# RWKV recurrence of a two-layer trunk: both heads' alpha and r in one tile, the keys' scores and the state apart, diagonal blocks in two parts

## Chip, cores and metric

The kernel runs on one core of a Trainium2 chip. The metric is the device time of one execution in microseconds. A run gives one time; a profile comes from one further execution.

## What is computed

A trunk of two layers on x of 1024 positions by 1024 channels. The first layer (gated spatial mixing beside dilated attention) is not touched. The second is RWKV-7 time mixing with 16 heads of 64 channels: projections of shifted inputs, then a recurrence over all positions, a norm of its output, a gate and an output projection. The recurrence is the part that matters here:

```python
def step(state, inp):
    r_t, w_t, k_t, v_t, kk_t, a_t = inp
    sa = jnp.einsum('bhvk,bhk->bhv', state, -kk_t)
    state = (state * w_t[:, :, None, :]
             + sa[..., None] * (kk_t * a_t)[:, :, None, :]
             + v_t[..., None] * k_t[:, :, None, :])
    y_t = jnp.einsum('bhvk,bhk->bhv', state, r_t)
    return state, y_t
```

## The kernel before

Everything is float32. The kernel does the recurrence in 16 chunks of 64 positions, all heads at once: 8 tiles q of two heads e each, on the partitions 64e to 64e+63. Of a chunk, A holds its alphas (the decayed removal keys) and r, BK its betas and keys. `scores` multiplies BK with both halves of A; ScalarE copies the r half into MY and the alphas' half, the keys' scores, into the other head's rows of A, so that one product over 128 rows, `W`, gives A-times-state plus scores-times-values. `alphas` gives the matrix M, which goes to DRAM (MA, `store_M`).

(1 + M) has to be inverted for each pair of chunks b. `load_M` brings M back, laid out for VectorE, into Nt: the same 64 rows of 4 KB go to the partitions 0 to 63 and 64 to 127. `inverse_a` forms DN from Nt and the norms rn (L1134) and solves the 8x8 diagonal blocks row by row, t = 1 to 7 (L1140 product, L1142 sum). `inverse_d` copies the blocks out, `inverse_b` does the block rows (L1165 to L1172), called one part at a time as `ib`. `inverse_c` stores the result to DRAM (XT, L1179), `load_X` brings it back (L1187), `merge_x` transposes it (`mx`, L1193, result rt), `merge_a` and `merge_b` (L1205, L1218) complete the inverse X on TensorE.

Then the chunks follow each other: `W` (L1230) gives Ws, `U` (L1240) multiplies it with X and puts the result beside the values in UV, `state` (L1261) adds BKT times UV (L1264) to what `keep` has scaled on GpSimd, and `Yout` (L1274) forms the output. State and values of a chunk share a tile SV, whose value half is loaded from DRAM (`load_sv`, L1031); UV's is loaded by `load_uv` (L1022).

The order is written by hand, in three strings: SCAN_START, six times SCAN_STEP (two chunks and one pair each) and SCAN_END. Each word calls one of these functions, and every engine and SP's DMA queue take their instructions in exactly that order. Work runs ahead: while chunks c and c+1 are finished, scores and alphas of c+4 and c+5 are made, M of pair b+2 is loaded and its diagonal blocks are solved, and the inverse of pair b+1 is merged. Between these, `g` places pieces of the gate's projection (L942, weights wraw split into wh and wl, L105 and L106; its results leave by a store sg_d on ScalarE's queue), of which ones with other inputs begin with the loads xh and xl. Tiles come from rings with a fixed number of buffers. DMAs count on eight shared completion counters, handed out in turn, so a DMA waits until the last one on its counter has landed.

Of the kernel before, what the change touches and what calls it, by code (L numbers as in the profile page):

```python
# [959 lines left out]

class Rwkv:
# [13 lines left out]
    def norms(self):  # L975

        g, nc, pool = self.g, self.g.nc, self.pool
        self.rn = rn = pool.tile([P, NB, 32], F32, name="rn")
        for c2 in range(2):
            for e in range(2):  # L980
                for b in range(2):
                    l0 = ((2 * e + b) * 2 + c2) * 8
                    src = bass.AP(tensor=g.ss_d.tensor, offset=g.ss_d.offset + e * KT * S + c2 * 64 + 32 * b,
                                  ap=[[S, 8], [128, NB], [1, 32]])
                    nc.scalar.dma_start(rn[l0:l0 + 8], src)

    def reciprocals(self, i):
        nc, rn = self.g.nc, self.rn
        nc.vector.tensor_scalar(rn[0:64], rn[0:64], 1e-24, None, op0=OP.max)
        nc.vector.reciprocal(rn[0:64], rn[0:64])  # L990
        nc.vector.tensor_copy(rn[64:128], rn[0:64])

    def ring(self, name, c, n, shape):
        k = name, c % n
        if k not in self.rings:
            if k == ("A1", NA - 1):
                self.rings[k] = self.pool.tile(shape, F32, name="Ax", bufs=1)
            else:
                self.rings[k] = self.g.s4(shape, F32, name)
        return self.rings[k]  # L1000

    def load(self, c):
        g, nc = self.g, self.g.nc
        A = []
        for e in range(2):
            rows, rest = slice(64 * e, 64 * e + 64), slice(64 - 64 * e, 128 - 64 * e)
            t = self.ring(f"A{e}", c, NA, [P, KT, 2, CH])
# [2 lines left out]
            nc.sync.dma_start(t[rows], g.A_d[rows, c])  # L1010
# [2 lines left out]
        nc.sync.dma_start(BK, g.BK_d[:, c])
        self.T[c] = dict(A=A, BK=BK)

    def load_uv(self, c):
        g, nc, pool = self.g, self.g.nc, self.pool
        UV = pool.tile([P, 2, KT, CH], F32, name="UV", bufs=2)
        v = g.v_d[c * CH:(c + 1) * CH]
        for e in range(2):  # L1020
            r = 64 - 64 * e
            nc.sync.dma_start(UV[r:r + 64, e].rearrange("t q d -> t (q d)"), v[:, e])  # L1022
        self.T[c]["UV"] = UV

    def load_sv(self, c):
        g, nc, pool = self.g, self.g.nc, self.pool
        v = g.v_d[c * CH:(c + 1) * CH]
        SV = pool.tile([P, 2, KT, CH], F32, name="SV", bufs=3)
        for e in range(2):
            r = 64 - 64 * e  # L1030
            nc.sync.dma_start(SV[r:r + 64, e].rearrange("t q d -> t (q d)"), v[:, e])  # L1031
        self.T[c]["SV"] = SV

    def scores(self, c, qq):
# [5 lines left out]
        pm = g.bB([P, 2, 4, 2, CH], "pm")  # L1042
        qs = slice(4 * qq, 4 * qq + 4)
        for i in range(4):
            q = 4 * qq + i
            for e in range(2):
                r = slice(64 * e, 64 * e + 64)
                nc.tensor.matmul(pm[:, e, i].rearrange("p j t -> p (j t)"), BK[r, q].rearrange("p j t -> p (j t)"),
                                 A[e][r, q].rearrange("p j t -> p (j t)"), start=True, stop=True)
        nc.scalar.activation(t["MY"].rearrange("p (e q) t -> p e q t", e=2)[:, :, qs], pm[:, :, :, 1], AF.Copy)  # L1050
        for e in range(2):
            r = slice(64 - 64 * e, 128 - 64 * e)
            nc.scalar.activation(A[e][r, qs, 0], pm[r, e, :, 0], AF.Copy)
# [52 lines left out]
    def load_M(self, b2):  # L1106
# [4 lines left out]
        for par in range(2):  # L1111
            nc.sync.dma_start(Nt[64 * par:64 * par + 64], g.MA_d[b2].rearrange("k c q t s -> (k c q) t s"))
        self.T[2 * b2]["Nt"] = Nf, Nt

    def inverse_p(self, b2):

        nc, pool = self.g.nc, self.pool
# [6 lines left out]
                              self.rn[:, b2].rearrange("p (k t) -> p k t", t=8))  # L1124
        self.blank = Xf, D, Nd

    def inverse_a(self, b2):
# [5 lines left out]
        r = self.rn[:, b2].rearrange("p (k t) -> p k t", t=8)  # L1133
# [119 lines left out]

    def state(self, c):
        g, nc, t = self.g, self.g.nc, self.T[c]
        if c < NC - 1:
# [5 lines left out]
            for e in range(2):  # L1262
                r = slice(64 * e, 64 * e + 64)
                nc.vector.tensor_tensor(self.T[c + 1]["SV"][r, e], pd[r], self.T[c + 1]["SV"][r, e], OP.add)  # L1264

    def Yout(self, c):
# [3 lines left out]
        for q in range(KT):  # L1270
            for a, b, first in (("MY", "UV", True), ("A", "SV", False)):
                for e in range(2):
                    w = t[a][:, 8 * e + q] if first else t[a][e][:, q, 1]
                    nc.tensor.matmul(py[64 * e:64 * e + 64, q], w, t[b][:, e, q], start=first, stop=not first)  # L1274
# [267 lines left out]
```

## Time and profile before

| | |
|---|---|
| median of 3 runs | 1496.92 us (1494.61 to 1498.73) |
| the profiled execution | 1504.67 us, of which span 1502.9 us |
| mean granted TensorE clock in it | 0.943 of full |
| TensorE, VectorE busy in the span | 89%, 62% |
| first layer | up to about 500 us |
| projections of the second | to about 987 us |
| recurrence (start, six steps, end) | about 987 to 1357 us |
| output projection, its tail | about 1357 to 1503 us |

A profile shows one execution: busy time of each engine, what each instruction waited for, DMA issues and packets. Engines: PE is TensorE, DVE VectorE, ACT ScalarE, POOL GpSimd, SP the engine that issues most DMAs. A name with q (SPq) is that engine's instruction queue. In a row of the timeline stand start, duration, engine, line, operation, tiles, and in brackets how long the engine stood idle before and what ended it.

### The profile page before, as it was taken

The numbers are of one execution on the slowest core, as the hardware profiler recorded it, in microseconds if no ns is written. First come the engines' busy times: TensorE is split into PE (matmuls) and PEld (weight loads), VectorE is DVE, ScalarE is ACT, GpSimd is POOL, SyncE is SP. The second block draws the span as 40 slices with busy tenths as digits, with TensorE's granted clock in tenths as the row PEclk, the third lists the DMA queues.
The fourth block names the chain that finished last, engine by engine and source line by source line (L and its number), as shares of the span: only waits on it lengthen the run. The fifth ranks groups of instructions, "written<-read, shape, count | busy, mean of one in ns | idle before, by whom it ended". The sixth has DMA issues, their size and how long they took to land.

```text
span 1502.9 us, 28032 instructions
## 1 busy us (share of the span) xinstructions
PE 1330.6 (89%) x11237; PEld 1130.5 (75%) x11237; DVE 933.2 (62%) x1504; ACT 645.2 (43%) x1236; POOL 565.1 (38%) x381
## 2 busy tenths in 40 slices
PE   5899999799989999999998779998878888978877
PEld 5887788688887799878754447996667777768777
DVE  8752536653565337650897898134577778777884
ACT  4422535543553234552654654134444444453322
POOL 9750102130114412211542543024654444477751
PEclk9999999899999999999998989999988999978998
DMA  6386436340523434142385557338486666765412
GB/s 217 85 273 174 126 117 165 80 131 8 168 78 115 139 127 139 36 150 78 88 250 145 121 150 187 78 98 237 110 256 171 163 158 163 204 207 197 153 31 98
DMA packets 256083, 213.19 MB, mean 142 GB/s; under 512 B 80416, under 2 KB 216192, under 8 KB 255952
## 3 DMA queue, kind: packets, MB, share of 16 engines
q1 hardware_dynamic: 232576, 196.11, 45.1%
q10 hardware_dynamic: 23376, 15.27, 3.8%
q8 instruction: 89, 1.46, 0.4%
q14 instruction: 42, 0.34, 0.1%
HBM read 139.90 MB, written 71.43 MB: 141 GB/s over the span
## 4 chain that ended last, share of the span: by engine, by line
PE 50%; DVE 19%; DMA 10%; ACT 7%; issue 7%; POOL 4%; SPq 3%; ACTq 0%; DVEq 0%; POOLq 0%
PE pj L153 33%; DVE tm L1140 2%; PE pt L572 2%; PE pj L1454 2%; PE pj L711 1%; PE pj L942 1%; DMA Nt<-MA 1%; DMA sg_d<-XT 1%; PE py L1274 1%; PE op L580 1%; ACT wh L105 1%; ACT xm L736 1%; DVE xm L737 1%; PE sp L559 1%; PE sp L562 1%
## 5 line engine op out<-in xcount | busy, mean ns | idle before, releaser
L106 POOL TENSOR_TENSOR wl<-wraw,wh 128x1024 fp32r<-128x1024 f32 x38 | 93.7, 2467 | 164.1 <-ACT wh L105 152.3
L106 DVE TENSOR_TENSOR wl<-wraw,wh 128x1024 fp32r<-128x1024 f32 x46 | 72.2, 1574 | 101.2 <-ACT wh L105 53.4
L153 PE MATMUL pj<-hh,wh 128*128 128x512 f32 x320 | 127.3, 398 | 0.0
L153 PE MATMUL pj<-hh,wl 128*128 128x512 f32 x320 | 126.6, 396 | 0.0
L153 PE MATMUL pj<-hl,wh 128*128 128x512 f32 x320 | 126.6, 396 | 0.0
L105 ACT ACTIVATE wh<-wraw 128x1024 fp32r<-128x1024 f32 x84 | 88.1, 1055 | 67.4 <-DMA wraw<-in_w_in_even_dram 23.0
L153 PE MATMUL pj<-xh,wh 128*128 128x512 f32 x256 | 103.4, 406 | 2.5 <-ACT ks L789 2.4
L153 PE MATMUL pj<-xl,wh 128*128 128x512 f32 x256 | 103.1, 403 | 2.6 <-DVE xl L740 2.6
L153 PE MATMUL pj<-xh,wl 128*128 128x512 f32 x256 | 102.7, 401 | 0.3 <-POOL wl L106 0.3
L566 DVE CUSTOM_DVE_ANT_0 sc<-sp,tb 128x128 f32<-128x128 f32 (+3 forms) x64 | 48.2, 754 | 56.7 <-PE sp L562 48.7
L1454 PE MATMUL pj<-wh,yh 128*128 128x256 f32 x256 | 76.0, 297 | 5.6 <-DVE x L1458 4.1
L1454 PE MATMUL pj<-wh,yl 128*128 128x256 f32 x256 | 75.0, 293 | 4.5 <-POOL yl L106 4.5
L737 DVE SCALAR_TENSOR_TENSOR xm<-hT,pr,xm 128x512 f32<-128x512 f32 x56 | 50.0, 935 | 45.2 <-ACT xm L736 44.8
L153 PE MATMUL pj<-wh,hh 128*128 128x256 f32 x256 | 74.8, 295 | 2.8 <-ACT hh L265 2.5
L153 PE MATMUL pj<-wh,hl 128*128 128x256 f32 x256 | 75.1, 294 | 1.2 <-DVE hl L266 1.2
L153 PE MATMUL pj<-wh,yl 128*128 128x256 f32 x256 | 73.7, 288 | 1.9 <-POOL yl L624 1.9
L1454 PE MATMUL pj<-wl,yh 128*128 128x256 f32 x256 | 74.6, 291 | 0.0
L153 PE MATMUL pj<-wl,hh 128*128 128x256 f32 x256 | 74.3, 291 | 0.0
L153 PE MATMUL pj<-wh,yh 128*128 128x256 f32 x256 | 73.2, 286 | 1.1 <-ACT yh L623 1.1
L153 PE MATMUL pj<-wl,yh 128*128 128x256 f32 x256 | 72.8, 284 | 0.0
L153 PE MATMUL pj<-wh,xh 128*128 128x256 f32 x256 | 72.2, 282 | 0.2
L153 PE MATMUL pj<-wl,xh 128*128 128x256 f32 x256 | 72.2, 282 | 0.0
(323 smaller groups left out, 4131.2 us busy)
## 6 DMA issues: line engine op xcount, KB each, us to landing
wraw<-in_w_in_even_dram SPq DMA_DIRECT2D x28, 512.0 KB
tb<-tb SPq DMA_DIRECT2D x16, 512.0 KB
A_d<-AR SPq DMA_DIRECT2D x16, 512.0 KB
wraw<-in_rw_wg_dram SPq DMA_DIRECT2D x16, 512.0 KB
BK<-BK_d SPq DMA_DIRECT2D x16, 512.0 KB
A<-A_d SPq DMA_DIRECT2D x30, 256.0 KB
xt<-in_x_dram SPq DMA_DIRECT2D x8, 512.0 KB
dv<-vt SPq DMA_DIRECT2D x16, 256.0 KB
```

The source lines that it names most:

```text
L105: nc.scalar.activation(hi, raw, AF.Copy)
L106: sub.tensor_tensor(lo, raw, hi.bitcast(F32), OP.subtract)
L153: nc.tensor.matmul(ps, a(k), b(k), start=(n == 0), stop=(n == 3 * KT - 1))
L559: nc.tensor.matmul(sp[:, c0:c1], qs[:, b * P:(b + 1) * P], kh[:, c0:c1], start=True, stop=False)
L562: nc.tensor.matmul(sp[:, c0:c1], qs[:, b * P:(b + 1) * P], kl[:, c0:c1], start=False, stop=True)
L566: nc.vector.tensor_tensor_reduce(sc[:, :n], sp[:, :n], tb[:, off:off + n], 1.0, BIG, OP.add, OP.min, mn)
L572: nc.tensor.transpose(pt[:, j - j0, :], sc[:, j * P:(j + 1) * P], g.ident)
L580: nc.tensor.matmul(op[:, s0:QW], vt[:, j, :], pth[j // 4][:, j % 4, s0:QW], start=(j == 0), stop=False)
L711: nc.tensor.matmul(ps, x[:, 2 * kk + i, :], y[:, i, o:o + 512], start=(n == 0), stop=(n == 47))
L737: nc.vector.scalar_tensor_tensor(t, hT[kk, f][:, j, 0:512], g.pr[:, i, k:k + 1], t, op0=OP.mult, op1=OP.add)
L1140: nc.vector.tensor_tensor(tv, D[:, :, 0:t, 0:t], Nd[:, :, t, 0:t][:, :, None, :].to_broadcast([P, 4, t, t]), OP.mult)
L1454: nc.tensor.matmul(ps[:, i, :], u[:, k], v[:, k % 4], start=(k == 0 and j == 0), stop=(k == KT - 1 and j == 2))
```

## The change

- A becomes one tile for both heads, loaded by one DMA of 512 KB instead of two of 256 KB; the zeroed halves and their memsets go.
- The keys' scores get a product `keys` of their own, with a tile AK; `scores` multiplies with r alone. W becomes two products, `Wkeys` (AK times UV, word V) and `W` (alphas times state).
- The state has a tile S; the value loads of SV go. `keep` and the state's addition are one operation each instead of two. UV has three buffers instead of two. `Yout` does all products of one kind, then all of the other.
- The two loads of Nt become one, whose source is a pattern that takes the same 64 rows twice (step 0, 2 times).
- The diagonal rows 5 to 7 move from `inverse_a`, ahead of `mx`, to `inverse_d`, behind it.
- The norms are loaded and inverted when the last keys have been projected, on SP's queue instead of ScalarE's.
- The three strings are written anew.

```diff
-FT = ((("BK", 3), ("BK", 3), ("BK", 3)), (("Nt", 1), ("tm", 1), ("SV", 3)), (("UV", 2), ("UV", 2), ("SV", 3)))
+FT = ((("BK", 3), ("BK", 3), ("BK", 3)), (("Nt", 1), ("tm", 1), ("FX", 1)), (("UV", 3), ("UV", 3), ("UV", 3)))
...
 SCAN_STEP = (
-    "U0 al0 ib2 st0 al1 sM0 sv0 Y0 keep1 ib1 W1 sc0 uv0 sv1 ib1 U1 sc1 ib1 ld6 ic0 dec0 st1 lM0 Y1 g1 W2 gx1 keep2 "
+    "U0 V1 al0 ib2 st0 al1 sM0 uv0 Y0 keep1 ib1 W1 sc0 ib1 U1 V2 ak0 uv1 ld6 st1 sc1 ib1 ic0 dec0 Y1 lM0 W2 keep2 ip0 "
...
+        if j == 9:
+            norms(g)
...
+def norms(g):
...
+            for b in range(2):
+                l0 = ((2 * e + b) * 2 + c2) * 8
+                src = bass.AP(tensor=g.ss_d.tensor, offset=g.ss_d.offset + e * KT * S + c2 * 64 + 32 * b,
+                              ap=[[S, 8], [128, NB], [1, 32]])
+                nc.sync.dma_start(rn[l0:l0 + 8], src)
+    nc.vector.tensor_scalar(rn[0:64], rn[0:64], 1e-24, None, op0=OP.max)
+    nc.vector.reciprocal(rn[0:64], rn[0:64])
+    nc.vector.tensor_copy(rn[64:128], rn[0:64])
...
     def load(self, c):
         g, nc = self.g, self.g.nc
-        A = []
-        for e in range(2):
-            rows, rest = slice(64 * e, 64 * e + 64), slice(64 - 64 * e, 128 - 64 * e)
-            t = self.ring(f"A{e}", c, NA, [P, KT, 2, CH])
-            if c < NA:
-                nc.gpsimd.memset(t[rest, :, 1], 0.0)
-            nc.sync.dma_start(t[rows], g.A_d[rows, c])
-            A.append(t)
+        A = self.ring("A", c, NA, [P, KT, 2, CH])
+        nc.sync.dma_start(A, g.A_d[:, c])
         BK = self.pool.tile([P, KT, 2, CH], F32, name="BK", bufs=3)
         nc.sync.dma_start(BK, g.BK_d[:, c])
         self.T[c] = dict(A=A, BK=BK)
     def load_uv(self, c):
         g, nc, pool = self.g, self.g.nc, self.pool
-        UV = pool.tile([P, 2, KT, CH], F32, name="UV", bufs=2)
+        UV = pool.tile([P, 2, KT, CH], F32, name="UV", bufs=3)
         v = g.v_d[c * CH:(c + 1) * CH]
         for e in range(2):
             r = 64 - 64 * e
             nc.sync.dma_start(UV[r:r + 64, e].rearrange("t q d -> t (q d)"), v[:, e])
         self.T[c]["UV"] = UV
-    def load_sv(self, c):
-        g, nc, pool = self.g, self.g.nc, self.pool
-        v = g.v_d[c * CH:(c + 1) * CH]
-        SV = pool.tile([P, 2, KT, CH], F32, name="SV", bufs=3)
-        for e in range(2):
-            r = 64 - 64 * e
-            nc.sync.dma_start(SV[r:r + 64, e].rearrange("t q d -> t (q d)"), v[:, e])
-        self.T[c]["SV"] = SV
...
     def scores(self, c, qq):
-        g, nc = self.g, self.g.nc
-        t = self.T[c]
+        g, nc, t = self.g, self.g.nc, self.T[c]
         A, BK = t["A"], t["BK"]
         if qq == 0:
             t["MY"] = self.ring("MY", c, NY, [P, NHD, CH])
-        pm = g.bB([P, 2, 4, 2, CH], "pm")
-        qs = slice(4 * qq, 4 * qq + 4)
+        pm = self.pm[:, :, qq]
         for i in range(4):
             q = 4 * qq + i
             for e in range(2):
                 r = slice(64 * e, 64 * e + 64)
-                nc.tensor.matmul(pm[:, e, i].rearrange("p j t -> p (j t)"), BK[r, q].rearrange("p j t -> p (j t)"),
-                                 A[e][r, q].rearrange("p j t -> p (j t)"), start=True, stop=True)
-        nc.scalar.activation(t["MY"].rearrange("p (e q) t -> p e q t", e=2)[:, :, qs], pm[:, :, :, 1], AF.Copy)
-        for e in range(2):
-            r = slice(64 - 64 * e, 128 - 64 * e)
-            nc.scalar.activation(A[e][r, qs, 0], pm[r, e, :, 0], AF.Copy)
+                nc.tensor.matmul(pm[:, e, i], BK[r, q].rearrange("p j t -> p (j t)"), A[r, q, 1], start=True, stop=True)
+        nc.scalar.activation(t["MY"].rearrange("p (e q) t -> p e q t", e=2)[:, :, 4 * qq:4 * qq + 4], pm, AF.Copy)
+    def keys(self, c):
+        g, nc, t = self.g, self.g.nc, self.T[c]
+        t["AK"] = AK = self.ring("AK", c // 2, 3, [P, 2, KT, CH])[:, c % 2]
+        pk = g.bC([P, KT, CH], "pt")
+        for q in range(KT):
+            for e in range(2):
+                r, o = slice(64 * e, 64 * e + 64), slice(64 - 64 * e, 128 - 64 * e)
+                nc.tensor.matmul(pk[o, q], t["BK"][r, q, 1 - e], t["A"][r, q, 0], start=True, stop=True)
+        nc.scalar.activation(AK, pk, AF.Copy)
     def alphas(self, c):
         g, nc, t = self.g, self.g.nc, self.T[c]
         M = self.ring("M", c // 2, 2, [P, 2, KT, CH])
-        pa = g.bA([P, KT, CH], "ch")
+        pa = g.bC([P, KT, CH], "pt")
         for q in range(KT):
             for e in range(2):
                 r = slice(64 * e, 64 * e + 64)
-                nc.tensor.matmul(pa[r, q], t["A"][e][r, q, 0], t["BK"][r, q, e], start=True, stop=True)
+                nc.tensor.matmul(pa[r, q], t["A"][r, q, 0], t["BK"][r, q, e], start=True, stop=True)
         nc.scalar.activation(M[:, c % 2], pa, AF.Copy)
...
-        for par in range(2):
-            nc.sync.dma_start(Nt[64 * par:64 * par + 64], g.MA_d[b2].rearrange("k c q t s -> (k c q) t s"))
+        m = g.MA_d[b2]
+        nc.sync.dma_start(Nf[:, 0:1024], bass.AP(tensor=m.tensor, offset=m.offset, ap=[[0, 2], [1024, 64], [1, 1024]]))
...
         self.T[2 * b2]["inv"] = Nt, X, D, Nd, Xf
-        for t in range(1, 8):
+        self.diag(D, Nd, 1, 5)
+    def diag(self, D, Nd, t0, t1):
+        nc = self.g.nc
+        for t in range(t0, t1):
...
     def inverse_d(self, b2):
         nc = self.g.nc
         Nt, X, D, Nd, Xf = self.T[2 * b2]["inv"]
+        self.diag(D, Nd, 5, 8)
...
+    def Wkeys(self, c):
+        g, nc, t = self.g, self.g.nc, self.T[c]
+        self.pw = g.bA([P, KT, CH], "ch")
+        for q in range(KT):
+            for e in range(2):
+                o, r = slice(64 * e, 64 * e + 64), slice(64 - 64 * e, 128 - 64 * e)
+                nc.tensor.matmul(self.pw[o, q], t["AK"][r, q], t["UV"][r, e, q], start=q == 0, stop=False)
     def W(self, c):
         g, nc, t = self.g, self.g.nc, self.T[c]
-        pw = g.bA([P, KT, CH], "ch")
         for q in range(KT):
             for e in range(2):
-                nc.tensor.matmul(pw[64 * e:64 * e + 64, q], t["A"][e][:, q, 0], t["SV"][:, e, q], start=True, stop=True)
-        nc.scalar.activation(self.Ws, pw, AF.Copy)
+                o = slice(64 * e, 64 * e + 64)
+                nc.tensor.matmul(self.pw[o, q], t["A"][o, q, 0], t["S"][o, q],
+                                 start=False, stop=q == KT - 1)
+        nc.scalar.activation(self.Ws, self.pw, AF.Copy)
...
+    def new_S(self, c):
+        S = self.pool.tile([P, KT, CH], F32, name="S", bufs=3)
+        self.T[c]["S"] = S
+        return S
     def keep(self, c):
-        g, t = self.g, self.T[c]
+        g = self.g
         if c < NC - 1:
-            for e in range(2):
-                r = slice(64 * e, 64 * e + 64)
-                g.nc.gpsimd.tensor_tensor(self.T[c + 1]["SV"][r, e], t["SV"][r, e],
-                                          g.EC[r, :, c:c + 1].to_broadcast([64, KT, CH]), OP.mult)
+            S = self.new_S(c + 1)
+            g.nc.gpsimd.tensor_tensor(S, self.T[c]["S"], g.EC[:, :, c:c + 1].to_broadcast([P, KT, CH]), OP.mult)
     def state(self, c):
         g, nc, t = self.g, self.g.nc, self.T[c]
...
                 for e in range(2):
                     r = slice(64 * e, 64 * e + 64)
                     nc.tensor.matmul(pd[r, q], t["BKT"][:, q, r], t["UV"][:, e, q], start=True, stop=True)
-            for e in range(2):
-                r = slice(64 * e, 64 * e + 64)
-                nc.vector.tensor_tensor(self.T[c + 1]["SV"][r, e], pd[r], self.T[c + 1]["SV"][r, e], OP.add)
+            S = self.T[c + 1]["S"]
+            nc.vector.tensor_tensor(S, pd, S, OP.add)
...
-            for a, b, first in (("MY", "UV", True), ("A", "SV", False)):
-                for e in range(2):
-                    w = t[a][:, 8 * e + q] if first else t[a][e][:, q, 1]
-                    nc.tensor.matmul(py[64 * e:64 * e + 64, q], w, t[b][:, e, q], start=first, stop=not first)
+            for e in range(2):
+                nc.tensor.matmul(py[64 * e:64 * e + 64, q], t["MY"][:, 8 * e + q], t["UV"][:, e, q],
+                                 start=q == 0, stop=False)
+        for q in range(KT):
+            for e in range(2):
+                r = slice(64 * e, 64 * e + 64)
+                nc.tensor.matmul(py[r, q], t["A"][r, q, 1], t["S"][r, q], start=False, stop=q == KT - 1)
         nc.scalar.activation(self.Y[:, c % 2], py, AF.Copy)
```

Where the strings move instructions, three places show it. The first is SP's queue at the Nt load of a steady step (sizes are those of the target; the name is target<-source). Before:

```order
L1010 DMA A_9498<-A_d 64x1024
L1010 DMA A_9501<-A_d 64x1024
L1013 DMA BK<-BK_d 128x1024
L1179 DMA XT_139<-xm 1024x1x32 x2
L1112 DMA Nt<-MA_132 64x1024 x2
L1187 DMA X<-XT_139 32x16x32 x4
L1022 DMA UV<-v_d 64x512 x2
L1010 DMA A_9581<-A_d 64x1024
```

And now:

```order
L1001 DMA A<-A_d 128x1024
L1003 DMA BK<-BK_d 128x1024
L1170 DMA XT_139<-xm 1024x1x32 x2
L1098 DMA Nt<-MA_132 128x1x1024
L1178 DMA X<-XT_139 32x16x32 x4
L1001 DMA A<-A_d 128x1024
L1003 DMA BK<-BK_d 128x1024
L928 DMA wraw<-in_rw_wg_dram 128x8x128
```

The load keeps its place between XT's store and X's loads, as one DMA; behind X now stands the next A, where UV's load stood.

The second is VectorE in the same step, from the block rows to the diagonal blocks. Before:

```order
L1165 TENSOR_TENSOR tm<-Nt,xm 128x576
L1167 TENSOR_REDUCE R<-tm 128x2x12
L1170 TENSOR_TENSOR tm<-DN,R 128x768
L1172 TENSOR_REDUCE xm<-tm 128x12x8
L1264 TENSOR_TENSOR SV<-ch,SV 64x512 x2
L106 TENSOR_TENSOR wl<-wraw,wh 128x1024
L1134 TENSOR_TENSOR DN<-Nt,rn 128x256
```

And now:

```order
L1156 TENSOR_TENSOR tm<-Nt,xm 128x576
L1158 TENSOR_REDUCE R<-tm 128x2x12
L1267 TENSOR_TENSOR S<-ch,S 128x512
L1161 TENSOR_TENSOR tm<-DN,R 128x768
L1163 TENSOR_REDUCE xm<-tm 128x12x8
L106 TENSOR_TENSOR wl<-wraw,wh 128x1024
L1120 TENSOR_TENSOR DN<-Nt,rn 128x256
```

The step's second addition to the state stands ahead of the last pair of row operations, after which XT is stored, instead of behind it.

The third is TensorE at the same place. Before, with the two A tiles taking turns in `scores` (eight rows in all behind U, of which two are shown):

```order
L1048 MATMUL pm<-A_9501,BK 128x128
L1240 MATMUL ch<-Ws,X 64x64 x16
L1048 MATMUL pm<-A_9498,BK 128x128
L1048 MATMUL pm<-A_9501,BK 128x128
...
L1261 MATMUL ch<-UV,BKT 64x64 x16
```

And now:

```order
L1029 MATMUL pm<-A,BK 128x64 x8
L1241 MATMUL ch<-Ws,X 64x64 x16
L1223 MATMUL ch<-UV,AK 64x64 x16
L1040 MATMUL pt<-A,BK 64x64 x16
L1265 MATMUL ch<-UV,BKT 64x64 x16
L1029 MATMUL pm<-A,BK 128x64 x8
```

Between U and the state's product (L1261, now L1265) stood half of a chunk's scores; now V (L1223) and the keys' product (L1040) stand there.

More of the change, by code (lines that the diff above doesn't have):

```diff
@@ L958, in pieces @@
                 yield
+def norms(g):
+    nc = g.nc
+    g.rn = rn = g.consts.tile([P, NB, 32], F32, name="rn")
+    for c2 in range(2):
+        for e in range(2):
[7 more added lines that the diff above has]
+    nc.vector.tensor_copy(rn[64:128], rn[0:64])
 class Rwkv:
@@ L973, in __init__ @@
         self.Ws = pool.tile([P, KT, CH], F32, name="Ws")
-    def norms(self):
-        g, nc, pool = self.g, self.g.nc, self.pool
-        self.rn = rn = pool.tile([P, NB, 32], F32, name="rn")
-        for c2 in range(2):
-            for e in range(2):
[L981 to L991, printed above, removed]
     def ring(self, name, c, n, shape):
@@ L995, in ring @@
         if k not in self.rings:
[L996 to L999, printed above, removed]
+            self.rings[k] = self.g.s4(shape, F32, name)
         return self.rings[k]
@@ L1095, in masks @@
                                     base=0, channel_multiplier=-1)
-        for e in range(2):
-            ak = t["A"][e][64 - 64 * e:128 - 64 * e, :, 0]
-            nc.gpsimd.affine_select(ak, ak, pattern=[[0, KT], [1, CH]], compare_op=OP.is_ge, fill=0.0,
+            nc.gpsimd.affine_select(t["AK"][r], t["AK"][r], pattern=[[0, KT], [1, CH]], compare_op=OP.is_ge, fill=0.0,
                                     base=-1, channel_multiplier=-1)
@@ L1123, in inverse_p @@
         nc.gpsimd.tensor_copy(D.rearrange("p k c t -> p k (c t)")[:, :, 0:64:9],
-                              self.rn[:, b2].rearrange("p (k t) -> p k t", t=8))
+                              g.rn[:, b2].rearrange("p (k t) -> p k t", t=8))
         self.blank = Xf, D, Nd
@@ L1132, in inverse_a @@
         X = Xf[:, 0:512].rearrange("p (c t) -> p c t", t=32)
[L1133 removed]
+        r = g.rn[:, b2].rearrange("p (k t) -> p k t", t=8)
         nc.vector.tensor_tensor(Nd, Nf.rearrange("p (k z) -> p k z", z=264)[:, :, 0:256]
@@ L1261, in state @@
                     nc.tensor.matmul(pd[r, q], t["BKT"][:, q, r], t["UV"][:, e, q], start=True, stop=True)
-            for e in range(2):
-                r = slice(64 * e, 64 * e + 64)
-                nc.vector.tensor_tensor(self.T[c + 1]["SV"][r, e], pd[r], self.T[c + 1]["SV"][r, e], OP.add)
+            S = self.T[c + 1]["S"]
+            nc.vector.tensor_tensor(S, pd, S, OP.add)
     def Yout(self, c):
@@ L1270, in Yout @@
         for q in range(KT):
-            for a, b, first in (("MY", "UV", True), ("A", "SV", False)):
-                for e in range(2):
-                    w = t[a][:, 8 * e + q] if first else t[a][e][:, q, 1]
-                    nc.tensor.matmul(py[64 * e:64 * e + 64, q], w, t[b][:, e, q], start=first, stop=not first)
+            for e in range(2):
+                nc.tensor.matmul(py[64 * e:64 * e + 64, q], t["MY"][:, 8 * e + q], t["UV"][:, e, q],
+                                 start=q == 0, stop=False)
+        for q in range(KT):
+            for e in range(2):
+                r = slice(64 * e, 64 * e + 64)
+                nc.tensor.matmul(py[r, q], t["A"][r, q, 1], t["S"][r, q], start=False, stop=q == KT - 1)
         nc.scalar.activation(self.Y[:, c % 2], py, AF.Copy)
@@ L1285, in zs @@
         def zs(i):
-            for e in range(2):
-                nc.gpsimd.memset(self.T[0]["SV"][64 * e:64 * e + 64, e], 0.0)
-        ops = dict(nm=self.reciprocals, L=gate.load, wx=gate.split, xl=gate.load_x, ld=self.load,
+            nc.gpsimd.memset(self.new_S(0), 0.0)
+        self.pm = g.bB([P, 2, 2, 4, CH], "pm")
+        ops = dict(L=gate.load, wx=gate.split, xl=gate.load_x, ld=self.load,
                    g=lambda i: [next(gate.rest, None) for _ in range(i)],
@@ L1294, in start @@
                    dec=self.decayed, T=self.transposed, msk=self.masks,
-                   sv=self.load_sv, uv=self.load_uv, W=self.W, keep=self.keep, zs=zs)
+                   ak=self.keys, uv=self.load_uv, V=self.Wkeys, W=self.W, keep=self.keep, zs=zs)
         for name, i in order(SCAN_START):
@@ L1302, in ops @@
             U=lambda i: self.U(c + i), st=lambda i: self.state(c + i), keep=lambda i: self.keep(c + i),
-            W=lambda i: self.W(c + i), sc=lambda i: self.scores(c + 4 + i // 2, i % 2),
+            W=lambda i: self.W(c + i), V=lambda i: self.Wkeys(c + i), sc=lambda i: self.scores(c + 4 + i // 2, i % 2),
             al=lambda i: self.alphas(c + 4 + i), sM=lambda i: self.store_M(b + 2 + i),
@@ L1311, in ops @@
             T=lambda i: self.transposed(c + 4 + i), Y=lambda i: self.Yout(c + i),
-            msk=lambda i: self.masks(c + 4 + i), sv=lambda i: self.load_sv(c + 2 + i),
+            msk=lambda i: self.masks(c + 4 + i), ak=lambda i: self.keys(c + 4 + i),
             uv=lambda i: self.load_uv(c + 2 + i), ld=lambda i: c + i < NC and self.load(c + i),
```

6 lines of the change are left out of this document (2 added, 4 removed), and 12 rows, old and new, of tables (SCAN_END, SCAN_START).

## The prediction

> **What bounds the kernel now.** I read the page's totals and its chain first, then the waits, grouped, of the recurrence's steady part (1104 to 1342 us), then one step's timeline on VectorE and on SP's queue.
>
> ```profile
> PE 1330.6 (89%) x11237; PEld 1130.5 (75%) x11237; DVE 933.2 (62%) x1504; ACT 645.2 (43%) x1236; POOL 565.1 (38%) x381
> ...
> PE 50%; DVE 19%; DMA 10%; ACT 7%; issue 7%; POOL 4%; SPq 3%; ACTq 0%; DVEq 0%; POOLq 0%
> ```
>
> TensorE is busy for 89% of the span, but the chain that ended last runs through TensorE for only half of it. The change touches the recurrence alone (about 987 to 1357 us), so what counts is what that stage waits for:
>
> ```profile
> PE pt L1218 <- DVE rt L1193: 26.1, 7, 4.5
> ...
> DVE SV L1264 <- PE ch L1261: 11.0, 10, 1.9
> DVE DN L1134 <- DMA Nt<-MA: 7.3, 5, 2.6
> ```
>
> The columns are total us, times, longest. TensorE's one large wait is `merge_b` (L1218) for the transposed inverse `rt` (L1193, `merge_x`), some 4 us in each step. So VectorE is late. Why, the timeline of the step from 1201 to 1237 us tells (start, duration, engine, line):
>
> ```profile
> 1201.17 0.70 DVE L1193 STREAM_TRANSPOSE rt<-X 128x512 f32<-128x512 f32 x1
> ...
> 1217.52 0.95 DVE L1172 TENSOR_REDUCE xm<-tm 128x96 f32<-128x768 f32 x1
> 1217.60 1.23 SPq L1010 DMA_DIRECT2D A<-A_d  x2
> 1218.93 0.53 SPq L1013 DMA_DIRECT2D BK<-BK_d  x1
> 1219.56 1.39 SPq L1179 DMA_DIRECT2D XT<-xm  x2
> 1220.05 1.41 DVE L1264 TENSOR_TENSOR SV<-ch,SV 64x512 f32<-64x512 f32 x2 [1.57 <-PE ch L1261]
> 1221.00 4.21 SPq L1112 DMA_DIRECT2D Nt<-MA  x2
> 1228.26 0.61 DVE L1134 TENSOR_TENSOR DN<-Nt,rn 128x256 f32<-128x256 f32 x1 [1.57 <-DMA Nt<-MA]
> ...
> 1234.55 0.95 DVE L1140 TENSOR_TENSOR tm<-DN 128x100 f32<-128x100 f32 x1
> 1237.26 0.70 DVE L1193 STREAM_TRANSPOSE rt<-X 128x512 f32<-128x512 f32 x1
> ```
>
> This is a loop, one turn per step. After `mx` (1201.17) come the block rows of the inverse, until 1218.47 (17.3 us). SP stores XT at 1219.56 (1.1) and, behind it in its queue, issues the Nt load at 1221.00 (1.4). VectorE, in its fixed order, stands at DN until Nt has landed, 1228.26 (7.3), and does the diagonal blocks before the next `mx` at 1237.26 (9.0). Sum 36.1 us. `mx` feeds TensorE's `mb`, and the next turn starts. From the second to the seventh `mx` there are five turns:
>
> ```profile
> 1128.54 0.70 DVE L1193 STREAM_TRANSPOSE rt<-X 128x512 f32<-128x512 f32 x1
> 1305.51 0.70 DVE L1193 STREAM_TRANSPOSE rt<-X 128x512 f32<-128x512 f32 x1
> ```
>
> That is 177.0 us, 35.4 each. The Nt load lies on this loop, and nothing hides a longer one: DN and what follows are next in VectorE's order.
>
> **The change, part by part.** First the part that I hold to decide. The two Nt loads of 64 rows become one of 128 rows, whose source is written as 2 copies of 64 rows. How many of the 16 DMA engines a transfer gets can be counted by the small packets that complete it:
>
> ```profile
> DMA packets 8, 0.01 MB, mean 5 GB/s; under 512 B 4, under 2 KB 4, under 8 KB 8
> ...
> ss_d<-so SPq DMA_DIRECT2D x1, 4.0 KB
> bo_d<-so SPq DMA_DIRECT2D x1, 4.0 KB
> ```
>
> ```profile
> DMA packets 544, 0.26 MB, mean 52 GB/s; under 512 B 32, under 2 KB 544, under 8 KB 544
> ...
> v_d<-rt SPq DMA_DIRECT2D x2, 128.0 KB
> ```
>
> ```profile
> q10 hardware_dynamic: 72, 0.01, 2.4%
> ...
> rn<-ss_d ACTq DMA_DIRECT2D x3, 8.0 KB
> ```
>
> In a quiet window (948.4 to 950.2) two stores of two 2 KB rows make 4 data and 4 small packets: two completions each. Two v_d stores (969 to 974) make 32: sixteen each. One rn load (all that ACT's queue q10 moved from 1010 to 1014) has 64 runs of 128 B, 8 KB, and the 72 packets leave 8 completions. It has 64 rows at its source, yet its target is written as 8 groups of 8 rows. So the outermost step of a pattern, not its rows or bytes, bounds the engines: 2, 8, 16. The new load's source has 2 in its outermost step, so I forecast **two engines**, with 64 rows of 4 KB each, where sixteen had 8 each in all.
>
> The page "DMA: Bandwidth & Descriptors" of the Trainium skill, section "Why a DMA increments its semaphore by 16 and not by 1", says the same as a rule: the engine count is the largest number up to 16 that divides the outermost dimension larger than one of both patterns, here of 128 and 2. That speaks against this change, and the three counts above agree with it; no run here shows it for a step of stride zero.
>
> What does an engine move in a microsecond?
>
> ```profile
> DMA packets 795, 2.90 MB, mean 414 GB/s; under 512 B 84, under 2 KB 88, under 8 KB 795
> ...
> q1 hardware_dynamic: 795, 2.90, 102.7%
> ```
>
> ```profile
> q1 hardware_dynamic: 484, 1.63, 96.3%
> ```
>
> From 13 to 20 us, loads of 4 KB rows keep sixteen engines full: 2.90 MB / 7 us / 16 = 25.9 GB/s each. From 1031 to 1038, with Nt and A loads, 1.63 MB / (7 us x 16 x 0.963) = 15.1 GB/s. An engine's share of the new load is 256 KB: 10.1 to 17.4 us, where an eighth of it took 1.3 to 2.2. **Added: 8.9 to 15.2 us per load.** I take 8.9: with fourteen engines idle it is nearer to the row without contention. The same page's "Specifications" gives some 27 GiB/s per engine; by that figure, an estimate, it would be 9.0 us per load instead of 10.1 and some 8 us less over the seven loads that count. The measured 25.9 decides.
>
> The loop's other terms in a steady step:
> - Rows: the last pair of row operations now stands behind the second state addition, and that behind W's key product V and the keys' product, which stand ahead of the state product on TensorE.
>
> ```profile
> 1216.11 1.15 PE L1240 MATMUL ch<-Ws,X 64*64 64x64 f32 x32
> 1217.69 1.16 PE L1048 MATMUL pm<-A,BK 64*128 64x128 f32 x16 [0.43 <-ACT A L1053]
> 1218.78 1.15 PE L1261 MATMUL ch<-UV,BKT 128*64 128x64 f32 x32
> ```
>
>   A group of 32 passes of 64x64 costs 1.15 us here, with 64 rows (first row) as with 128 (last). U ends at 1217.3; V and keys 2.3; state 1.15; the addition, now one 128x512 operation, 0.7 (half of the 1.41 above); the last pair 1.94: 1223.4, less 0.7 for the first addition, which is halved too: 1222.7, so 21.6 us after `mx` instead of 17.3. **+4.3.** Not hidden: the XT store waits for it. If V and keys ran in others' shadow, it would be +2.
> - XT issue: A and BK have been issued long before, 0.3 instead of 1.1: -0.8. XT to Nt stays 1.4.
> - Nt without the penalty: 7.3, of which the 2 us of A and BK issued just ahead no longer stand in front, nor the rest of that queue: 4.4 (3.5 to 7.3), -2.9.
> - Diagonal rows 5 to 7 go behind `mx`: 1237.26 - 1234.55 = 2.7 less. The remaining 6.3 hold operations that took 0.9 and more for a handful of elements while POOL worked; later in a longer step POOL has finished: 5.0 (4.6 to 6.3), -4.0 in all.
>
> Sum: 21.6 + 0.3 + 1.4 + 4.4 + 5.0 = 32.7 us, and with 8.9 for the two engines **41.6**. Against 35.4 that is +6.2, five times: **+31**.
>
> The start pays twice:
>
> ```profile
> 1038.24 1.49 DVE L1134 TENSOR_TENSOR DN<-Nt,rn 128x256 f32<-128x256 f32 x1 [13.99 <-DMA Nt<-MA]
> ...
> 1066.77 1.26 SPq L1179 DMA_DIRECT2D XT<-xm  x2
> 1068.21 1.31 SPq L1112 DMA_DIRECT2D Nt<-MA  x2
> 1070.40 2.17 SPq L1187 DMA_DIRECT2D X<-XT  x4
> 1075.02 0.71 DVE L1193 STREAM_TRANSPOSE rt<-X 128x512 f32<-128x512 f32 x1 [8.28 <-DMA X<-XT]
> ```
>
> VectorE stands idle 14 us for the first Nt, then works without a gap until XT goes out: +8.9 passes through. The second Nt stands ahead of the X loads in the same queue, and `mx` waits for X: on the two engines X's share comes behind Nt's, +8.9 again. The first `mx` moves from 1075.0 to 1092.8. From it to the second there were 53.5 us, 18.1 more than a turn, of which these waits go:
>
> ```profile
> ACT UV L1243 <- DMA xh<-xg: 7.9, 1, 7.9
> ...
> ACT MY L1050 <- DMA XT<-xm: 8.6, 1, 8.6
> ```
>
> ScalarE was held behind two stores of the gate, whose completion counters are shared with a load; the counters fall otherwise now. What is late next: wraw behind X, and A and BK behind the eight gate loads of 512 KB. I keep 10 of the 18 (3 to 18). The second `mx` comes at 1092.8 + 41.6 + 10 = 1144.4: **+16** (+6 to +25).
>
> The rest I cost at nothing:
>
> ```profile
> 1201.20:1237.30 36.10, 31.03 (x619) 26.38 (x619) 27.17 (x42) 16.99 (x32) 16.77 (x17) 0.91 0.64 166
> ...
> SPq L1022 <- PE py L1274: 80.8, 5, 17.4
> ```
>
> The first row is the same turn by engine (length, then PE's busy time, weight loads, DVE, ACT, POOL, then the granted clock, the DMA share and GB/s). SV's 32 loads, the memsets and SP's long wait for Y (second row) go, but they were off the loop: the queue held back loads, not VectorE. On TensorE, scores without the alphas' half save half of 1.16 us four times, 2.3; keys and V, two groups each per turn, add 4 x 1.15, 4.6: 31.0 becomes 33.3, hidden while a turn takes 41.6 and the bound if a turn could be shorter. From the last of the five turns to the tail no Nt load follows: -2 (-5 to +3) for the halved additions. The tail is unchanged.
>
> Sum: 31 + 16 - 2 = **+45** on the profiled execution's 1504.67 us (span 1502.9), so 1549.7. It ran 7.75 us above the median of 1496.92; taken off, **1542 us**.
>
> **Rivals.**
> 1. *All sixteen engines serve the load* (the outermost step of stride zero is folded away, or the target's 128 rows decide). For it: the loads before, of 64 rows, were short, and the trace has no transfer with a repeated source. Against it: rn, whose 8 rather than 64 set the count. The loop is then 32.7 us, so TensorE's 33.3 binds: -2.1 five times, -10.5; the start loses the two ScalarE waits in part, -8; the end -2: -20.5, 1476 us, **faster**. It decides from where seven loads eat that gain, 2.9 us more each than before: 512 KB in 4.2 us, that is five engines at 25.9 GB/s.
> 2. *Two engines, and slow ones*: 15.1 GB/s as from 1031 to 1038, where the same source rows were read. Then 6.3 us more per load, seven times: +44, 1586 us.
> 3. *The queue behind the load binds*: SP's next BK load waits for the completion counter that Nt uses, and A, BK, wraw and UV stand behind it. For it: SP's queue is in order. Against: they are wanted only in the next step's first products, some 6 us after `mx`. If 3 us late: +15, 1557 us.
>
> **How the numbers follow.** Forecast 0.61 (1517 to 1562: loop 39 to 44, start +6 to +25), rival 2 0.14, rival 3 0.10, rival 1 0.11, something between (some five engines, about no change) 0.04. The likeliest is 1542. The range leaves out rival 1 and the upper part of rival 2: 1508 to 1576. A measurement of this kernel can tell 0.3%, 4.5 us, from no change: faster 0.11, same 0.04, slower 0.85.
>
> **What would show it.** Right: VectorE's wait for Nt (DN, now L1120) of some 8 to 10 us in each step; stretches of ten us in which the DMA share is about a tenth or two (2 of 16 engines) while Nt is in flight; `mx` (L1184) 41 to 42 us apart, and TensorE's wait for it over 8 us; the first `mx` near 1093. An XT store 21 to 22 us after `mx` confirms the rows' term. Wrong: Nt landing within 5 us of its issue and `mx` 33 to 34 us apart (rival 1), or `mx` 48 apart (rival 2), or first products after `mb` waiting for BK or UV (rival 3).

## The result, and the profile after

The changed kernel takes 1544.34 us (median of 4 runs, 1541.35 to 1551.85) beside 1495.76 us before (4 runs, 1490.02 to 1498.73): ratio 1.0337, 95% interval 1.0288 to 1.0386. It is slower by some 49 us. The profiled execution took 1541.35 us. The ratios, here and below, are not the quotients of the two medians, and two executions at a low granted clock (1743 us at 0.69, 1962 us at 0.60) are not in them.

The page of the changed kernel, busy times and chain:

```profile
PE 1349.7 (88%) x12261; PEld 1154.1 (75%) x12261; DVE 885.2 (57%) x1489; ACT 631.7 (41%) x1188; POOL 545.9 (35%) x353
...
PE 57%; DVE 15%; DMA 10%; issue 5%; ACT 5%; POOL 3%; SPq 3%; ACTq 1%; DVEq 0%; POOLq 0%
PE pj L153 34%; PE pj L943 3%; DMA X<-XT 3%; SPq L1178 2%; PE pj L1460 1%; PE pt L572 1%; PE pj L711 1%; PE pm L1029 1%; DMA BK<-BK_d 1%; DMA Nt<-MA 1%; PE pt L1051 1%; PE sp L559 1%; PE ch L1241 1%; PE sp L562 1%; PE op L580 1%
```

VectorE and GpSimd do less than before, and the kernel is longer: the time is waited for. The chain now names the loads of X at 3% and SP's issuing of them (L1178) at 2%, which it did not before. The grouped waits of the recurrence (1104 to 1380 us; total, times, longest) say on what:

```profile
PE pt L1196 <- DMA X<-XT: 42.9, 8, 9.0
...
PE pt L1209 <- ACT rt L1199: 4.0, 2, 3.7
...
DVE DN L1120 <- DMA Nt<-MA: 64.8, 6, 11.5
DVE S L1267 <- PE ch L1265: 37.5, 12, 6.4
```

VectorE waits 64.8 us for Nt, where it was 7.3 for the five loads shown of before, and TensorE waits at `merge_a` (L1196) for X. A wait of TensorE's `merge_b` (L1209) for VectorE's transpose, 26.1 us before, is no longer among its waits; the 4.0 us at L1209 are for a copy on ScalarE. The turn of the loop from 1125.75 to 1169.05, on VectorE, SP and TensorE:

```profile
1125.75 0.70 DVE L1184 STREAM_TRANSPOSE rt<-X 128x512 f32<-128x512 f32 x1
...
1148.15 0.69 DVE L1267 TENSOR_TENSOR S<-ch,S 128x512 f32<-128x512 f32 x1 [5.86 <-PE ch L1265]
1149.74 0.95 DVE L1163 TENSOR_REDUCE xm<-tm 128x96 f32<-128x768 f32 x1
1150.72 1.27 SPq L1170 DMA_DIRECT2D XT<-xm  x2
1152.09 0.56 SPq L1098 DMA_DIRECT2D Nt<-MA  x1
1154.36 8.96 SPq L1178 DMA_DIRECT2D X<-XT  x4
1166.87 0.42 DVE L1120 TENSOR_TENSOR DN<-Nt,rn 128x256 f32<-128x256 f32 x1 [11.09 <-DMA Nt<-MA]
1167.41 0.28 PE L1196 MATMUL pt<-X,M 32*32 32x32 f32 x2 [8.41 <-DMA X<-XT]
1169.05 0.70 DVE L1184 STREAM_TRANSPOSE rt<-X 128x512 f32<-128x512 f32 x1
1174.25 1.20 PE L1209 MATMUL pt<-rt 32*32 32x32 f32 x64
```

Nt lands 14.8 us after its issue, where it was 7.3. Of X's four loads the first goes out 2.3 us behind Nt and the last 10.8 us: SP is 8.96 us at their issue, where it was 1.9 in the turn of before that the prediction shows. X is there some 1 us after Nt. How many engines carry Nt stands in the DMA view of 1157 to 1166 us, whose digits are the mean busy share of the 16 engines in tenths:

```profile
DMA  9899989811111111111111111101296693110111
GB/s 246 200 246 209 246 189 195 169 56 55 55 55 55 55 55 46 55 46 55 55 55 55 55 55 46 64 36 73 62 182 137 123 223 67 61 55 36 55 55 39
```

For some 4 us on end the queues move a steady 55 GB/s, at a share of one tenth, while Nt is in flight. Two of 16 engines full are 0.125, and 55 GB/s on two are some 27 each, beside the 25.9 that the forecast took from the row of 13 to 20 us.

### The profile page after: what moved, and what is told of

It reads as the page before. It is cut to its first block, busy times and chain, and to the rows that moved or that the text cites. A ratio compares the mean times of both kernels' runs of the same rounds, so it can differ in the third digit from the quotient of the medians.

```text
span 1539.6 us, 29856 instructions
## 1 busy us (share of the span) xinstructions
PE 1349.7 (88%) x12261; PEld 1154.1 (75%) x12261; DVE 885.2 (57%) x1489; ACT 631.7 (41%) x1188; POOL 545.9 (35%) x353
## 4 chain that ended last, share of the span: by engine, by line
PE 57%; DVE 15%; DMA 10%; issue 5%; ACT 5%; POOL 3%; SPq 3%; ACTq 1%; DVEq 0%; POOLq 0%
PE pj L153 34%; PE pj L943 3%; DMA X<-XT 3%; SPq L1178 2%; PE pj L1460 1%; PE pt L572 1%; PE pj L711 1%; PE pm L1029 1%; DMA BK<-BK_d 1%; DMA Nt<-MA 1%; PE pt L1051 1%; PE sp L559 1%; PE ch L1241 1%; PE sp L562 1%; PE op L580 1%
## 5 line engine op out<-in xcount | busy, mean ns | idle before, releaser
L1460 PE MATMUL pj<-wl,yh 128*128 128x256 f32 x256 | 75.5, 295 | 0.0
L153 PE MATMUL pj<-wh,xl 128*128 128x256 f32 x256 | 72.8, 284 | 0.0
```

What stands on the lines that cost most here:

```text
L153: nc.tensor.matmul(ps, a(k), b(k), start=(n == 0), stop=(n == 3 * KT - 1))
L1460: nc.tensor.matmul(ps[:, i, :], u[:, k], v[:, k % 4], start=(k == 0 and j == 0), stop=(k == KT - 1 and j == 2))
```

## The experiments

Each ran beside the kernel before, on the same chip. A turn below is the mean of the five from the second to the seventh transpose `mx` in the profiled execution.

**Two loads of 64 rows again.** In the changed kernel only this:

```diff
-        nc.sync.dma_start(Nf[:, 0:1024], bass.AP(tensor=m.tensor, offset=m.offset, ap=[[0, 2], [1024, 64], [1, 1024]]))
+        for par in range(2):
+            nc.sync.dma_start(Nt[64 * par:64 * par + 64], g.MA_d[b2].rearrange("k c q t s -> (k c q) t s"))
```

> The whole change, but Nt again loaded by two DMAs of 64 rows (as before the change). Theory (the one load runs on two DMA engines, and that is what costs): each of the two completes on 16 engines, Nt lands some 4 to 5 us after the issue of the first instead of 14.4, the merges (transposes of X on VectorE) come 33 to 35 us apart instead of 42.7, and the time is 1476 us, 1462 to 1490: faster than before the change. Rival (the rest of the change costs the time, later block rows, or W's second product): it stays above 1520, with merges over 40 us apart.

1495.0 us, ratio to before 0.9971 (0.9944 to 0.9999). The load explains all of the loss; but the time is above the expected range, and the rest of the change, for which 1476 was expected, gains only some 3 to 4 us. The same places of the loop, one turn from 1152.3 to 1188.07:

```profile
1173.45 0.69 DVE L1268 TENSOR_TENSOR S<-ch,S 128x512 f32<-128x512 f32 x1 [4.65 <-PE ch L1266]
...
1176.02 1.52 SPq L1171 DMA_DIRECT2D XT<-xm  x2
...
1177.64 1.27 SPq L1099 DMA_DIRECT2D Nt<-MA  x2
...
1182.60 0.52 DVE L1121 TENSOR_TENSOR DN<-Nt,rn 128x256 f32<-128x256 f32 x1 [1.53 <-DMA Nt<-MA]
...
1188.07 0.70 DVE L1185 STREAM_TRANSPOSE rt<-X 128x512 f32<-128x512 f32 x1
```

Nt lands 5.0 us after its issue, and X's four loads go out in 2.2 us. A turn is 35.9 us instead of 42.7, but no shorter than before (35.4): VectorE stands 4.65 us for the second addition to the state, and the last pair of block rows, and so XT, behind it. That made the rows' place the next suspect.

**The kernel before with the one load**, the same edit the other way round:

> The kernel before, with nothing changed but that Nt is loaded by the one DMA of two copies. Theory: VectorE waits for Nt in each step, merges 42 to 44 us apart instead of 35.4, and 1540 us, 1525 to 1560: about all that the whole change added comes from this one line. Rival (the load is only slow together with the rest): within 10 us of 1496.

1526.3 us, ratio 1.0206 (1.0161 to 1.0251): slower, inside the expected range at its low end, but the expected turns of 42 to 44 us didn't come. A turn is 38.4 us, +3.0 where the changed kernel has +6.8 from the same line. On VectorE:

```profile
1167.41 0.81 DVE L1134 TENSOR_TENSOR DN<-Nt,rn 128x256 f32<-128x256 f32 x1 [9.37 <-DMA Nt<-MA]
1172.31 0.70 DVE L1193 STREAM_TRANSPOSE rt<-X 128x512 f32<-128x512 f32 x1
```

From DN to `mx` it takes 4.9 us where it was 9.0; the diagonal rows now run after most of GpSimd's work of the step rather than beside it (that GpSimd is the cause is inferred from the times). And TensorE, which before waited 26.1 us in seven times for `mx` and 0.2 for X, now waits for X and not for `mx`; its one large wait from 1132 to 1325 us is

```profile
PE pt L1205 <- DMA X<-XT: 28.5, 7, 6.7
```

So a part of X's delay, some 4 us a step, only takes the place of the wait for `mx`.

**Patterns of 2 and of 8 rows outermost, without a repeat.** Two DMAs of 64 rows, the rows in another order (for 8: steps 1024 by 8, 8192 by 8):

```diff
-        nc.sync.dma_start(Nf[:, 0:1024], bass.AP(tensor=m.tensor, offset=m.offset, ap=[[0, 2], [1024, 64], [1, 1024]]))
+        for par in range(2):
+            nc.sync.dma_start(Nf[64 * par:64 * par + 64, 0:1024], bass.AP(tensor=m.tensor, offset=m.offset, ap=[[1024, 2], [2048, 32], [1, 1024]]))
```

> The whole change, with two DMAs of 64 rows for Nt, each of whose source patterns is written as 2 times 32 rows with no step of zero (rows 0, 2, 4 ... and then 1, 3, 5 ...): the rows of M come in another order, so the output isn't the reference's. Theory (the outermost number of a pattern is the number of engines): 2 completions for each of the two, both on the same two engines, Nt lands 14 us after issue as in the changed kernel, merges 42 to 43 us apart, 1535 to 1550. Rival (taking the same rows twice at once is slow, step zero): as with the two loads of plain rows, some 1476 and 34 us apart.

> As the one before with 8 times 8 rows in place of 2 times 32 (rows in another order, output not the reference's). Theory: 8 completions for each of the two; an engine's share is 64 KB at about 25 GB/s, 2.6 us instead of 1.3, so Nt lands 1 to 3 us later than with two plain loads of 64 rows, merges 34 to 37 us apart, and 1478 to 1500. Rival (any pattern with more than one step of rows is slow): as with 2 times 32, over 1530.

One run each: 1555.3 us with 2 outermost, 1501.1 with 8, 5 and 1 us above the expected ranges. With 2, the DMA view of 1162 to 1176 us has the same tenths in long stretches, though no row is taken twice by one DMA:

```profile
DMA  0315999821111931111111112998676751111117
GB/s 12 94 47 126 222 210 223 206 66 47 47 59 47 174 77 36 59 53 47 47 59 59 47 47 76 252 222 199 164 154 127 125 101 41 42 49 31 29 16 72
```

With 8, from 1145 to 1157 us, the share while Nt is in flight reads 5 at first and then mixes with other loads:

```profile
DMA  5999031555899979588989999998999998998999
...
Nt<-MA SPq DMA_DIRECT2D x2, 256.0 KB
```

VectorE's wait for six loads of Nt is 73.7 us with 2, 26.8 with 8, and 10.9 with the two plain loads. The turns are 44.2 us with 2 and 35.9 with 8, no longer than with the plain loads. So the outermost number sets the engines, step of zero or not; the rival, that reading the same rows twice is what is slow, falls.

**The last block rows ahead of the second addition** (two loads; one word of the step moved):

```diff
-    "U0 V1 al0 ib2 st0 al1 sM0 uv0 Y0 keep1 ib1 W1 sc0 ib1 U1 V2 ak0 uv1 ld6 st1 sc1 ib1 ic0 dec0 Y1 lM0 W2 keep2 ip0 "
+    "U0 V1 al0 ib2 st0 al1 sM0 uv0 Y0 keep1 ib1 W1 sc0 ib1 U1 ib1 V2 ak0 uv1 ld6 st1 sc1 ic0 dec0 Y1 lM0 W2 keep2 ip0 "
```

> Two loads of 64 rows for Nt, and the last pair of block rows ahead of the second addition to the state on VectorE, as it was before the change (in the two-loads kernel VectorE waits some 4 us for that addition in each step, and the store of XT with it). Theory (that wait took back what the rest of the change saves): the wait leaves the loop, XT goes out 4 us sooner after the merge, and a turn falls from 35.9 us to about TensorE's own work, 32.7 busy, so 33.3: five turns -13, 1482 us, 1474 to 1490. Rival (TensorE is the bound already, busy for 91% of those turns): within 5 us of 1495.

1474.06 us, ratio 0.9854 (0.9833 to 0.9874), the best of all, 22 us faster than before, so the rival falls. The turn is 31.6 us, less than the 33.3 expected. In the windows of the five turns (length, then PE's busy time, weight loads, DVE, ACT, POOL, granted clock, DMA share, GB/s), here and in the kernels before and changed:

```profile
1116.60:1274.50 157.90, 152.56 (x3680) 135.88 (x3680) 120.92 (x191) 76.36 (x129) 74.59 (x74) 1.00 0.61 157
```

```profile
1128.50:1305.50 177.00, 153.12 (x3087) 130.56 (x3087) 134.85 (x201) 83.22 (x157) 83.53 (x84) 0.91 0.64 160
```

```profile
1125.70:1339.30 213.60, 167.49 (x3704) 148.08 (x3699) 103.20 (x192) 75.83 (x129) 69.86 (x70) 0.87 0.44 118
```

TensorE is now busy for 97% of the turns, at the full clock. Its busy time for 3680 matmul records, 152.56 us, is that of 3087 records before at a mean clock of 0.91 (153.12): what the added products cost, the higher clock gives back. That the clock is higher because TensorE hardly stands idle fits all three rows, but no run separates the two.

**The same with XT's store and Nt's load moved up in SP's queue as well**, ahead of the next values, A and BK:

```diff
-U1 ib1 V2 ak0 uv1 ld6 st1 sc1 ic0 dec0 Y1 lM0 W2
+U1 ib1 ic0 lM0 V2 ak0 uv1 ld6 st1 sc1 dec0 Y1 W2
```

> As the one before, with the store of XT and the load of Nt also moved up in SP's queue, ahead of the next loads of values, A and BK. Theory: XT goes out right behind the last block row and no load stands ahead of it; 1480 us, 1470 to 1490, no slower than the one before. Rival (X, now behind A and BK, is late next): TensorE waits longer for X at the merge, turns of 35 us or more, 1490 or more.

1481.15 us, ratio 0.9902 (0.9881 to 0.9922): in the expected range, but slower than the kernel just before, not as fast as it, so the theory missed. The turn is 32.7. The rival's cause, that X is waited for, doesn't show either: TensorE waits 0.9 us for it in those turns. Its busy time there is longer, 156.6 us for 3685 records beside 152.6 for 3680. Why stays open.

**The diagonal rows together again** (two loads):

```diff
-        self.diag(D, Nd, 1, 5)
+        self.diag(D, Nd, 1, 8)
...
-        self.diag(D, Nd, 5, 8)
```

> Two loads of 64 rows for Nt, and the diagonal rows 5 to 7 back ahead of the merge's transpose, as before the change. Theory (in the two-loads kernel TensorE does not wait for that transpose but for X, its transpose on TensorE and what stands between): the transpose comes 2.7 us later after DN, of which 2 are hidden; 1495 to 1502. Rival (VectorE's path to the transpose is the loop, as it was before): 2.7 us in each of six turns, 1511.

1501.96 us, at the upper end of the expected range, ratio 1.0040 (1.0020 to 1.0061), beside 0.9971 with the rows apart. The turn is 37.5 instead of 35.9. So 1.6 of the 2.7 us count, more than the theory has (0.7 of it), less than the rival; TensorE waits for the transpose again (11.9 us in five times). By the two ratios, moving rows 5 to 7 behind `mx` is worth 0.7%, some 10 us.

**The kernel before with the norms early.** The changed kernel's `norms`, called there as there, and nothing else:

```diff
+        if j == 9:
+            norms(g)
...
-    rw.norms()
```

> The kernel before, with nothing changed but the norms: their eight loads on SP's queue when the last keys have been projected, instead of on ScalarE's at the start of the recurrence. Theory (the changed kernel's first load of Nt went out 10 us sooner because of this): the first load of Nt goes out near 1020 us instead of 1030, the first merge comes near 1066 instead of 1075, and 1487 us, 1482 to 1493. Rival (A as one tile, no memsets, or alphas in other buffers did that): within 4 us of 1496, first load of Nt near 1030.

1496.63 us, ratio 1.0008 (0.9990 to 1.0026): no difference clear of noise, so the theory missed. The time is the rival's, but its cause isn't shown by it. The first Nt goes out at 1026.74 instead of 1030.15, so the norms are 3.4 of the 10 us by which it goes out sooner in the changed kernel; where the others come from is said at the start's step below.

**The one load kept, the last rows first:**

```diff
-U1 V2 ak0 uv1 ld6 st1 sc1 ib1 ic0 dec0
+U1 ib1 V2 ak0 uv1 ld6 st1 sc1 ic0 dec0
```

> The changed kernel, its one load of Nt kept, with the last pair of block rows ahead of the second addition to the state. Theory (the load and the late rows lie one behind the other on one loop, so each can be taken away by itself): XT goes out some 4.5 us sooner after the merge's transpose, turns fall from 42.7 to 38 us, and with the end's step 1517 us, 1508 to 1528. Rival (VectorE's long stand at the load covers the wait for the addition, so that only the load counts): turns within 1.5 us of 42.7, 1536 or more.

1513.37 us, ratio 1.0134 (1.0093 to 1.0174); the turn is 37.7. The expectation, 38 and 1517, holds, and the rival falls. The four kernels make a square: rows late 1544.3 and 1495.0 (one load, two loads), rows first 1513.4 and 1474.1, each beside a median before of 1495.8 to 1497.8. The load costs 49 or 39 us, the rows' place 31 or 21 (by the ratios some 55 or 42, and 30 or 18): both lie on the loop.

## Why the prediction was right, step by step

The forecast was 1542 us, the median 1544.34. The cause was the one named, two engines for the load. The path by which it costs the time was another than the prediction's loop, and the sizes nearly cancel, so the last two us are luck.

- **Two engines: right.** The share of 0.1, the 55 GB/s and the two patterns without a repeat show it. The price of 8.9 us per load was about right in size: from issue to DN 14.8 us in the turn above, where the sum had 4.4 + 8.9 = 13.3.
- **The path: not the one forecast.** The prediction lets the late Nt reach TensorE through DN, the diagonal rows and `mx`, and names as a sign that TensorE waits over 8 us for `mx`. That wait is gone. The chain that ended last, from the turn above into the next, runs through SP's issue of X's loads and X's landing; beside it the same place of the kernel with two loads of 64 rows, the first experiment:

```profile
1157.43 5.36 SPq L1178
1162.84 5.06 DMA X<-XT
1167.94 1.91 PE pt L1196 x62
```

```profile
1179.76 2.22 SPq L1179 DMA_DIRECT2D X<-XT  x4
```

  From the last issue X takes 5.1 us, as with two loads (4.9, from 1181.20 to 1186.13). What differs is the issue, 8.96 us instead of 2.22, of which the third load's alone takes 6.0: +6.7, and the turn is +6.8. In four of the five turns the chain goes through that issue, for 3.4 to 5.7 us, in the fifth through one of X's loads that lands 10.4 us after its issue. VectorE's 11 us at DN are beside the chain; it has 5.86 us to spare at the second addition.
- **The turn: 42.7 us, forecast 41.6.** VectorE's round adds up in the turn shown, 25.0 + 1.4 + 14.8 + 2.2 = 43.3 against the forecast's 21.9 + 1.4 + 13.3 + 5.0, but only because its waits for TensorE are in it. From `mx` to XT's issue the sum had 21.9, and it took 24 to 26. The late rows' term in it, +4.3, was right: with the rows first a turn is 4.3 us shorter with two loads and 5.0 with the one. What was not in it: TensorE runs dry at `merge_a` and then works at half its clock. TensorE's windows in the changed kernel, of two stretches behind the wait for X (length, then PE's busy time with its records, granted clock, DMA share, GB/s):

```profile
1169.90:1174.20 4.30, 4.30 (x14) 0.52 0.85 242
1174.30:1178.00 3.70, 3.70 (x83) 1.00 0.02 4
```

  Six records of the gate's projection and eight of BK's transpose take 4.3 us at 0.52, and `mb` comes 5.2 us after `mx` where it came 0.9 after. The Trainium skill's page "TensorE: Matmul & The Clock Gate", Part 1, has the array fall to half rate after an idle window of some 3.4 us; the 8.41 us of idle above and the 0.52 agree. From DN to `mx` the sum had 5.0 and it took 2.2: with GpSimd done, the first diagonal row's product took 0.17 us instead of 0.9.
- **The start: the step that was mis-sized most.** It forecast the first `mx` at 1092.8 and the second 16 us late; they came at 1077.4 and 1125.75, the second 2.8 us *sooner* than before.

```profile
1020.25 0.57 SPq L1098 DMA_DIRECT2D Nt<-MA  x1
```

```profile
1034.87 0.42 DVE L1120 TENSOR_TENSOR DN<-Nt,rn 128x256 f32<-128x256 f32 x1 [35.65 <-DMA Nt<-MA]
...
1077.41 0.71 DVE L1184 STREAM_TRANSPOSE rt<-X 128x512 f32<-128x512 f32 x1 [16.14 <-DMA X<-XT]
```

  Both of its delays are there: Nt lands 14.6 us after its issue instead of 8.1, and the wait for X is 16.14 instead of 8.28. But it let the first load go out at 1030 as before, and it went out at 1020. Most of these 10 us lie ahead of the change. The last store of `ss_d`, in the projections ahead of all that was changed, stands 6.8 us apart in the two profiles, before and after:

```profile
948.51 0.23 SPq L826 DMA_DIRECT2D ss_d<-so  x1
```

```profile
941.73 0.23 SPq L826 DMA_DIRECT2D ss_d<-so  x1
```

  The first store of the first layer's result is already 6.3 us apart (527.90 and 521.59). The kernel before with the one load, whose code up to there is the same as before, has the `ss_d` store at 944.13: 4.4 of the 6.8 us lie between two executions of the same code, and no run tells whether the rest does. Counted from that store the first load goes out 3.1 us sooner, about what the norms gave alone, and the second `mx` comes 4.0 us *later*, where the forecast had 16.
- **From the last turn to the end:** forecast -2. `mx` to `mx` took 40.0 instead of 35.4, +4.7, of which only a part is explained: ScalarE was held 6.4 us for a store of Y whose counter it had to wait for, where it stood 4.45 at the same place before. The tail is 1.8 us shorter.
- **The sum.** In the two profiled executions: -2.8 to the second `mx`, +36.6 for five turns (213.6 against 177.0), +4.7, -1.8: +36.7, as the spans say (1539.6 against 1502.9), where the forecast had +45. Without the 6.8 us that the two executions differ by ahead of the change it is +43.5. The medians differ by 48.6, since the profiled execution before was 8.9 us above its median and the one after 3.0 below it.
- **Rivals.** The first, sixteen engines, is what two loads show: its mechanism is excluded in the changed kernel, and its price of 1476 was too low, at 1495.0. It had the turns 10.5 us shorter in all, and they were 2.5 longer (35.9 each instead of 33.3): `mx` to XT's issue took 23.7 us in the turn shown, where the sum had 21.9, and the other terms 0.2 to 0.6 more each. With the rows first the kernel does reach 1474. The second, slow engines, falls with 55 GB/s on two. The third, the queue behind the load, is a part of what happened: SP's queue is held, but at X, and not at BK or UV.

## What to carry to other kernels

Joining two transfers into one saved some 0.7 us of issue here and cost a multiple of it: look at the outermost step of both patterns, and keep a large number there; a repeat of two put in front left two engines. Then ask of each loaded tile whether the loop goes through it, and what stands behind it in the same queue: here the tile behind it, X, was the one that TensorE waited for. And an operation put ahead of the one that starts a store or load delays all of that loop: moving one word, the last block rows ahead of an addition, was worth some 20 us.

## What the runs showed of the hardware

- A transfer's engines go by the outermost number of its pattern also where its step is zero (one load of two copies) and where it has another step (2 and 8): Nt's landing follows, with VectorE's waits over six loads of 73.7 us for 2, 26.8 for 8 and 10.9 for 64.
- A transfer on few engines held up the queue behind it. SP was 6.9 to 9.0 us at the issue of X's four loads behind the one load of Nt, 7.0 to 11.6 us with 2 outermost, 1.9 to 3.4 with 8 and 1.9 to 2.2 with the two plain loads. In the turn shown the third load's issue takes 6.0 us, with no semaphore wait of that length in the trace. What it waits for there isn't shown.
- A lower clock came with the waiting: TensorE's busy time for nearly the same work in five turns was 167.5 us at a mean clock of 0.87, and 152.6 at 1.00.
